# Seven products for eight in one round of a convolutional feed-forward layer, with a factor sum made in place and modulation steps at a shorter pause

## The chip, the cores and the metric

One core of a Trainium2 chip runs the whole program. The time is device microseconds of one execution. Each engine of the core (PE, the multiplying engine; DVE, the vector engine; ACT, the scalar engine; POOL, the general engine; SP, which starts transfers) takes its instructions from a queue of its own, in the order in which the program has them. An instruction waits for semaphores that others raise, and everything behind it on its engine waits too.

## The reference

The program is a small network on one sequence of 512 positions with 1,024 features: a recurrent mixer, a feed-forward layer with a convolution, an attention mixer, a second such feed-forward layer, then a gated feed-forward layer, a hybrid mixer and another gated feed-forward layer. What matters here is the feed-forward layer with a convolution, used twice, its gated sister, and the modulation:

```python
def conv_ffn(h, w_up, conv_w, conv_b, w_down):
    a, v = jnp.split(h @ w_up, 2, axis=-1)
    a = lax.conv_general_dilated(a, conv_w[:, None, :].astype(a.dtype), window_strides=(1,),
                                 padding=[(CONV_W - 1, 0)], dimension_numbers=('NWC', 'WIO', 'NWC'),
                                 feature_group_count=D_FF) + conv_b
    return (jax.nn.silu(a) * v) @ w_down

def swiglu(x, w_gu, w_down):
    g, u = jnp.split(x @ w_gu, 2, axis=-1)
    return (jax.nn.silu(g) * u) @ w_down
...
    for layer in range(DEPTH):
        mod = c_act @ ada_w[layer] + ada_b[layer]
```

The inner width is 2,816, that is 22 tiles of 128; the convolution goes over three positions (the current one and two before it), each feature by itself. All data are 32-bit floats. The modulation of a layer is a vector (the activated condition) times a matrix of 1,024 x 6,144.

## The kernel before

Every large product is made of three products of shorter numbers. A weight block is split on ACT into a high part (line 241) and on DVE into the low part that is left (line 242); the activations are split in the same way (lines 465 and 468). PE adds high x high, high x low and low x high in a bank (lines 354, 355 and 357, called plain below; 455 to 457 where seven products are used).

**Weights.** All blocks of the program stand in one list. SP loads each into one of six slots called raw (512 KB); tasks split it into one of six pairs of buffers, wh and wl, so that up to six split blocks wait for PE. A slot is free when its block has been split.

**Order of the work.** There is no scheduler behind the code. While the Python code emits PE's instructions it adds up a modelled time (`wv.pe`), and side tasks that have come due are run in between and emit theirs: splits, evictions, modulation. A task says with `yield` how many modelled microseconds later it goes on. So where an instruction stands in its engine's queue follows from these delays; when it runs is settled on the chip by the queues and semaphores.

**The feed-forward layers** go over the inner tiles in three rounds, tiles 0 to 6, 6 to 14 and 14 to 22. In each round, pairs of tiles are multiplied up (the a half and the v half), evicted into two buffers mh and ml (the split inner activations), and four blocks of the down product follow. In the convolutional layers a pair is evicted tile by tile: `ev_a` applies the weight of the current position and the bias on ACT (line 1151), adds the two earlier positions on DVE (line 1153) and takes the Silu on ACT (line 1164); `ev_v` multiplies by v (line 1169) and splits.

**Seven products.** In the gated layers from tile 4 on, a pair of tiles is a group of seven products of half the rows and half the positions (`fm_fast`), in place of eight. Positions 0 to 255 and 256 to 511 and the upper and lower half of the 1,024 inputs make a 2 x 2 scheme: of the weights come the factors A11, A12, A22, S1, S2, S3, S4, of the activations the inputs X and the sums T, which `fast_inputs` makes once a layer on DVE (lines 404 and 424 to 427, then a split). S1 is A21 + A22, S2 is S1 + A11, S3 is A11 + A21, S4 is A12 + S2. The products are added in three banks A, E and F; bank A is used by A11, S2, S3 and A22 in turn, and ACT copies it out in between (lines 1111 and 1117). S1 and S3 are summed by loading one block and adding the other with a transfer that accumulates (line 197, issued by POOL); S2 and S4 are summed on DVE (lines 212 and 215), S2 in a buffer of its own.

**Modulation of the second layer** is made during the first convolutional layer by `ada_rest`: for each of twelve column blocks of 512, eight steps on DVE (line 694, then 696), one weight row-block each (loaded by ACT's queue, line 738), each step followed by a pause; four transposes on PE (line 674) and a reduction on DVE (line 676) end the block.

Of the kernel before, what the change touches and what calls it, by code (L numbers as in the profile page):

```python
# [20 lines left out]
S = 512  # L21
# [7 lines left out]
T_D, FAST_FROM, SCRATCH = 1.8, 4, 4096  # L29
# [12 lines left out]
ADA_LAG, ADA_PACE, ADA_START, ADA_PACE0 = 1.8, 2.0, 22.8, 1.5  # L42
# [7 lines left out]

GL_D = (5.0, 4.0, 4.8, 2.2, 2.0)
# [67 lines left out]
class Builder:  # L119
# [35 lines left out]
    FACTORS = ("A11", "A12", "S2", "S1", "S3", "S4", "A22")  # L155

    def w_init(self, items):
        self.loads, self.pieces, self.item_pieces = [], [], []
        self.groups = {}
        for it in items:  # L160
            first = len(self.pieces)
            if it[0] == "S":
# [5 lines left out]
                self.loads += [(a21, a22), (a11,), (a12,), (a11, a21), (a22,)]  # L168
# [17 lines left out]
    def w_dma(self):  # L186

        while self.w_dma_i < len(self.loads) and self.w_dma_i < self.w_freed + RAW_BUFS:
            i = self.w_dma_i
            self.w_dma_i += 1  # L190
            raw = self.t([128, 4, 256], "raw", RAW_BUFS)
            for n, (ap, r0, nk, c0, ncol) in enumerate(self.loads[i]):
                src = ap[r0 * 128:(r0 + nk) * 128, c0:c0 + ncol].rearrange("(k p) m -> p k m", p=128)
                if n == 0:
                    self.nc.sync.dma_start(raw[:, :nk, :ncol], src)
                else:
                    self.nc.gpsimd.dma_start(raw[:, :nk, :ncol], src, accum_op=OP.add)
            self.w_raw[i] = raw

# [4 lines left out]
    PARTS = dict(S1=0, A11=1, A12=2, S3=3, A22=4, S4=2)  # L204

    def w_sum(self, g, name):
# [3 lines left out]
        if name == "S2":  # L210
            g["S2"] = self.t([128, 4, 256], "wsum")
            tt(g["S2"], raw("S1"), raw("A11"), op=OP.add)
            self.raw_free()
        else:
            tt(raw("A12"), raw("A12"), g["S2"], op=OP.add)
# [5 lines left out]
    def w_split(self, i, slow=True):  # L221
# [8 lines left out]
        else:  # L230
            g = p["g"]
            load = g["load"] + self.PARTS.get(kind, 0)
            yield from self.w_wait_load(load)
            src = g["S2"] if kind == "S2" else self.w_raw[load]
# [12 lines left out]
        if kind in ("raw", "S1", "S3", "S4", "A22"):  # L247
            self.raw_free()
        elif kind == "A11":
            self.w_sum(g, "S2")  # L250
        elif kind == "A12":
            self.w_sum(g, "S4")
# [142 lines left out]
    def fast_inputs(self, X, tags, first, second):  # L395
# [12 lines left out]
        def run():  # L408
            yield from self.wv.wait_in(first)
            yield 1.5  # L410
# [22 lines left out]
    def fm_fast(self, X, T, blocks, after):  # L433
# [4 lines left out]
        steps = (("A11", x(0, 0), "A"), ("A12", x(4, 0), "F"), ("S2", t(4, 0), "A"), ("S1", t(0, 0), "E"),  # L438
# [629 lines left out]
    def ffn_blocks(self, up, down, fast=False):  # L1068
        out = []
        for a, b in self.ROUNDS:  # L1070
            for t in range(a, b, 2):
                pair = [(up, 0, 8, t * 128, 256), (up, 0, 8, DFF + t * 128, 256)]
                out += [("S", *pair)] if fast and t >= FAST_FROM else pair
# [3 lines left out]
    def ffn(self, X, waits, up, down, scale, after, conv=None, tags=None):  # L1077
# [4 lines left out]
        fast = tags is not None  # L1082
        if fast:
            T, t_task = self.fast_inputs(X, tags, *waits)
        pend = []

        def fast_group(a, t):
# [42 lines left out]
            self.fm_fast(X, T, ((up, 0, 8, t * 128, 256), (up, 0, 8, DFF + t * 128, 256)), after)  # L1130

        for r, (a, b) in enumerate(self.ROUNDS):
            mh, ml = self.big("b0", F32R), self.big("b1", F32R)
            for t in range(a, b, 2):
# [37 lines left out]
                if fast and t >= FAST_FROM:  # L1172
# [776 lines left out]
    def blocks(self):  # L1949
# [9 lines left out]
        out += self.ffn_blocks(I["ffn_w_up"][0], I["ffn_w_down"][0])  # L1959
# [4 lines left out]
        out += self.ffn_blocks(I["ffn_w_up"][1], I["ffn_w_down"][1])  # L1964
        out += self.ffn_blocks(I["ffn1_w_gu_2"][0], I["ffn1_w_down_2"][0], True)
        out += self.hy_blocks()
        out += self.ffn_blocks(I["ffn2_w_gu_2"][0], I["ffn2_w_down_2"][0], True)
        return out

    def conv_ffn(self, X, waits, layer, after):  # L1970
# [3 lines left out]
        self.ffn(X, waits, I["ffn_w_up"][layer], I["ffn_w_down"][layer], self.m(layer, 5), after, (cw, cb))  # L1974
# [35 lines left out]
    def build(self, stop=99):  # L2010
# [55 lines left out]
        self.conv_ffn(st["X"], st["tasks"], 0, begin1)  # L2066
# [13 lines left out]
        self.conv_ffn(st["X"], st["tasks"], 1, begin2)  # L2080
        if stop == 4:
            for t in self.st2["tasks"]:
# [4 lines left out]
                 tags=("b2", "b3"))  # L2087
# [11 lines left out]
        def begin_out():  # L2099
# [4 lines left out]
            def after(lo, hi):  # L2104
# [3 lines left out]
                 tags=("b2", "b3"))  # L2108
# [22 lines left out]
```

## Time and profile before

| | |
|---|---|
| median of three runs | 2736.74 us (2731.54 to 2738.49) |
| the profiled execution | 2735.41 us |
| its span | 2733.7 us |
| mean granted clock of PE | 0.994 |
| PE busy | 2685.7 us, 98% |
| DVE busy | 1637.7 us, 60% |
| ACT busy | 1143.7 us, 42% |
| POOL busy | 325.2 us, 12% |

The span is the time between the first and the last event that the profiler saw; the execution's own time is a little longer. Of the stages that the change touches, the first convolutional layer goes from about 378 to 760 us: up products of round one until 446, of round two from 480 to 568, of round three from about 615 to 703, each followed by down products. The gated layers go from about 1485 to 1838 and from 2380 to the end. In a timeline row the number behind the shape is the count, and the bracket holds the idle time of the engine just before and what ended it. In a grouped row the sum and the mean in ns stand before the last bar, and behind it the idle time and what ended most of it.

### The profile page before, as it was taken

To read this page: it belongs to the slowest core of one execution; us is meant where nothing else is said; L and a number is where in the kernel's file an instruction comes from. 1 tells how busy PE (TensorE), PEld (TensorE's weight loads), DVE (VectorE), ACT (ScalarE), POOL (GpSimd) and SP (SyncE) were. 2 spreads that over 40 slices of the span, in tenths; PEclk is the share of its full clock that TensorE was granted. 3 is DMA by queue.
4 is the path that set the end of the run, shared out by engine and by line. 5 is a ranking of instruction groups with operands and counts; after the bars stand their busy time and mean duration, and the time that the engine had idled before them with its cause. 6 is when DMAs were issued, how large, how long until landed. Compare 5 with 4: busy or idle time off the path is not lost.

```text
span 2733.7 us, 40282 instructions
## 1 busy us (share of the span) xinstructions
PE 2685.7 (98%) x15857; PEld 2346.6 (86%) x15857; DVE 1637.7 (60%) x2945; ACT 1143.7 (42%) x2114; POOL 325.2 (12%) x440
## 2 busy tenths in 40 slices
PE   6999999999999999999999999999999999999999
PEld 5988898888877888888889898997878987989898
DVE  7866567767553797644446774753456234577574
ACT  3323343323333696433234443543256333344353
POOL 3111110000101594000002000010000000101001
PEclk8999999999999999999999999999999999999999
DMA  7642126565241002232332564747535432357461
GB/s 265 187 152 86 55 67 209 177 189 172 85 116 62 9 2 63 72 114 93 93 99 70 142 168 128 184 69 116 98 81 82 72 82 88 85 139 170 131 171 54
DMA packets 286170, 307.25 MB, mean 112 GB/s; under 512 B 17272, under 2 KB 260365, under 8 KB 285981
## 3 DMA queue, kind: packets, MB, share of 16 engines
q1 hardware_dynamic: 239243, 242.67, 32.2%
q10 hardware_dynamic: 27730, 43.14, 5.2%
q0 software_dynamic: 19008, 18.88, 4.7%
q8 instruction: 125, 2.05, 0.3%
q14 instruction: 64, 0.52, 0.1%
HBM read 302.54 MB, written 2.10 MB: 111 GB/s over the span
## 4 chain that ended last, share of the span: by engine, by line
PE 91%; DVE 5%; ACT 2%; issue 1%; POOL 1%; ACTq 0%; DVEq 0%; POOLq 0%
PE pg L354 21%; PE pg L355 21%; PE pg L357 21%; PE pg L456 4%; PE pg L457 4%; PE pg L455 4%; PE pa L883 2%; PE pg L386 1%; PE pg L384 1%; PE pg L385 1%; PE pa L1488 1%; DVE w L696 1%; DVE wl L242 1%; PE pa L510 1%; DVE w L526 1%
## 5 line engine op out<-in xcount | busy, mean ns | idle before, releaser
L242 DVE TENSOR_TENSOR wl<-raw,wh 128x512 fp32r<-128x512 f32 (+2 forms) x824 | 613.5, 770 | 337.6 <-ACT wh L241 336.3
L354 PE MATMUL pg<-b,wh 128*128 128x512 f32 (+1 forms) x1856 | 673.4, 364 | 1.0 <-DVE w L1169 1.0
L355 PE MATMUL pg<-b,wl 128*128 128x512 f32 (+1 forms) x1856 | 668.1, 361 | 0.0
L241 ACT ACTIVATE wh<-raw 128x512 fp32r<-128x512 f32 (+2 forms) x824 | 515.8, 667 | 300.3 <-PE pg L357 136.9
L357 PE MATMUL pg<-b,wh 128*128 128x512 f32 (+1 forms) x1472 | 522.5, 357 | 0.0
L354 PE MATMUL pg<-hTh,wh 128*128 128x512 f32 (+2 forms) x1096 | 410.9, 377 | 2.4 <-ACT hTh L465 1.2
L355 PE MATMUL pg<-hTh,wl 128*128 128x512 f32 (+2 forms) x1096 | 405.1, 371 | 0.7 <-DVE wl L242 0.7
L354 PEld LDWEIGHTS pg<-b,wh 128*128 128x128 f32 x1856 | 348.6, 188 | 57.1 <-DVE w L1169 1.4
L357 PE MATMUL pg<-hTl,wh 128*128 128x512 f32 (+2 forms) x1096 | 396.3, 368 | 0.0
L355 PEld LDWEIGHTS pg<-b,wl 128*128 128x128 f32 x1856 | 348.8, 188 | 54.6
L357 PEld LDWEIGHTS pg<-b,wh 128*128 128x128 f32 x1472 | 275.1, 188 | 43.7
L354 PEld LDWEIGHTS pg<-hTh,wh 128*128 128x128 f32 (+1 forms) x1096 | 205.5, 187 | 46.6 <-issue 4.6
L357 PEld LDWEIGHTS pg<-hTl,wh 128*128 128x128 f32 (+1 forms) x1096 | 202.3, 187 | 40.6 <-DVE hTl L468 0.4
L355 PEld LDWEIGHTS pg<-hTh,wl 128*128 128x128 f32 (+1 forms) x1096 | 205.5, 187 | 35.6 <-DVE wl L242 1.1
L487 POOL TENSOR_TENSOR w<-w,w 128x256 f32<-128x256 f32 (+1 forms) x78 | 78.0, 1005 | 1222.6 <-ACT w L486 1222.0
L455 PE MATMUL pg<-b,wh 128*128 128x256 f32 x576 | 160.9, 279 | 1.3 <-ACT w L1111 1.3
L457 PE MATMUL pg<-b,wl 128*128 128x256 f32 x576 | 161.3, 280 | 0.0
L456 PE MATMUL pg<-b,wh 128*128 128x256 f32 x576 | 160.7, 279 | 0.0
L465 ACT ACTIVATE b<-w 128x512 fp32r<-128x512 f32 (+1 forms) x92 | 54.4, 594 | 235.8 <-DVE w L1169 149.7
L357 PE MATMUL pg<-hTh,wh 128*128 128x512 f32 (+1 forms) x384 | 142.9, 378 | 0.0
L456 PE MATMUL pg<-hTl,wh 128*128 128x256 f32 x432 | 122.6, 284 | 0.0
L455 PE MATMUL pg<-hTh,wh 128*128 128x256 f32 x432 | 121.3, 281 | 0.0
(414 smaller groups left out, 4218.0 us busy)
## 6 DMA issues: line engine op xcount, KB each, us to landing
raw<-in_ffn_w_gu_dram SPq DMA_DIRECT2D x106, 512.0 KB
raw<-in_ffn_w_up_dram SPq DMA_DIRECT2D x88, 512.0 KB
w<-in_ada_w_dram ACTq DMA_DIRECT2D x160, 256.0 KB
raw<-in_ffn_w_down_dram SPq DMA_DIRECT2D x64, 512.0 KB
raw<-in_w_in_dram SPq DMA_DIRECT2D x64, 512.0 KB
raw<-in_ffn_w_gu_dram POOLq DMA_DIRECT2D x36, 512.0 KB, 6.5
raw<-in_hg_w_in_dram SPq DMA_DIRECT2D x32, 512.0 KB
raw<-in_ffn_w_down_dram SPq DMA_DIRECT2D x32, 384.0 KB
```

Of the source, the lines that this page charges most:

```text
L241: nc.scalar.activation(h[:, k:e, :ncol], src[:, k:e, :ncol], AF.Copy)
L242: nc.vector.tensor_tensor(l[:, k:e, :ncol], src[:, k:e, :ncol], h[:, k:e, :ncol].bitcast(F32), op=OP.subtract)
L354: mm(p[:mw, :n], h[:, c], xh[:, k, lo:hi], start=k == 0, stop=False)
L355: mm(p[:mw, :n], l[:, c], xh[:, k, lo:hi], start=False, stop=False)
L357: mm(p[:mw, :n], at(j)[0][:, c], xl[:, j, lo:hi], start=False, stop=j == nk - 1)
L384: mm(p[:, :n], xh[:, k, tk], h[:, :n], start=k == 0, stop=False)
L455: mm(o, h[:, k, c], xh, start=first and k == 0 and m == 0, stop=False, skip_group_check=True)
L456: mm(o, h[:, k, c], xl, start=False, stop=False, skip_group_check=True)
L457: mm(o, l[:, k, c], xh, start=False, stop=k == 3 and m == 1, skip_group_check=True)
L465: self.nc.scalar.activation(h, src, AF.Copy)
L487: nc.gpsimd.tensor_tensor(acc[0][:, lo:hi], acc[0][:, lo:hi], sq[:, lo:hi], op=OP.add)
L883: mm(p[:, c, :n], s["k"][:, cc], q, start=True, stop=True)
```

## The change

It does four things.

The first convolutional layer's third round (tiles 14 to 22, four groups) uses seven products. `FAST_FROM` is now a table by layer. The eviction of such a group is new: `after_conv` adds the parts of a in a buffer, `convolve` applies the convolution to both tiles, and `out_conv` gates and splits. The sums T of this layer are made later in the layer by a delay of 190 modelled us.

In all groups of seven the order of the factors is A11, S1, S2, A12, S3, S4, A22, and products and weights follow it. S2 is summed in S1's slot; A21 is then added to A11's slot by an accumulating transfer, which makes S3 there. A group loads four slots and six blocks, where it was five slots and seven blocks.

The modulation's pause is 1.3 modelled us for 2.0.

```diff
-T_D, FAST_FROM, SCRATCH = 1.8, 4, 4096
+T_D, SCRATCH = 1.8, 4096
-ADA_LAG, ADA_PACE, ADA_START, ADA_PACE0 = 1.8, 2.0, 22.8, 1.5
+ADA_LAG, ADA_PACE, ADA_START, ADA_PACE0 = 1.8, 1.3, 22.8, 1.5
+FAST_FROM = (14, None, 4, 4)
+T_DELAY = 190.0
...
-    FACTORS = ("A11", "A12", "S2", "S1", "S3", "S4", "A22")
+    FACTORS = ("A11", "S1", "S2", "A12", "S3", "S4", "A22")
...
-                self.loads += [(a21, a22), (a11,), (a12,), (a11, a21), (a22,)]
+                g["a21"] = a21
+                self.loads += [(a21, a22), (a11,), (a12,), (a22,)]
...
+    def w_load(self, raw, block, add=False):
+        ap, r0, nk, c0, ncol = block
+        src = ap[r0 * 128:(r0 + nk) * 128, c0:c0 + ncol].rearrange("(k p) m -> p k m", p=128)
+        if add:
+            self.nc.gpsimd.dma_start(raw[:, :nk, :ncol], src, accum_op=OP.add)
+        else:
+            self.nc.sync.dma_start(raw[:, :nk, :ncol], src)
...
-    PARTS = dict(S1=0, A11=1, A12=2, S3=3, A22=4, S4=2)
+    PARTS = dict(S1=0, A11=1, A12=2, A22=3, S2=0, S3=1, S4=2)
...
         if name == "S2":
-            g["S2"] = self.t([128, 4, 256], "wsum")
-            tt(g["S2"], raw("S1"), raw("A11"), op=OP.add)
-            self.raw_free()
-        else:
-            tt(raw("A12"), raw("A12"), g["S2"], op=OP.add)
+            tt(raw("S1"), raw("S1"), raw("A11"), op=OP.add)
+            self.w_load(raw("A11"), g["a21"], True)
+        else:
+            tt(raw("A12"), raw("A12"), raw("S2"), op=OP.add)
+            self.raw_free()
...
-        steps = (("A11", x(0, 0), "A"), ("A12", x(4, 0), "F"), ("S2", t(4, 0), "A"), ("S1", t(0, 0), "E"),
+        steps = (("A11", x(0, 0), "A"), ("S1", t(0, 0), "E"), ("S2", t(4, 0), "A"), ("A12", x(4, 0), "F"),
                  ("S3", t(0, 256), "A"), ("S4", x(4, 256), "E"), ("A22", t(4, 256), "A"))
...
+            def convolve():
+                x, y = c["a"], c["y"]
+                w = lambda j, m: cw[:, j * FT + t + m:j * FT + t + m + 1]
+                yield 1.0
+                for m in range(2):
+                    nc.scalar.activation(y[:, m], x[:, m], AF.Identity, scale=w(2, m), bias=cb[:, t + m:t + m + 1])
+                yield 1.6
+                for m in range(2):
+                    for j, d in ((1, 1), (0, 2)):
+                        nc.vector.scalar_tensor_tensor(y[:, m, d:], x[:, m, :S - d], w(j, m), y[:, m, d:],
+                                                       op0=OP.mult, op1=OP.add)
+                    yield 1.7
+                nc.scalar.activation(y, y, AF.Silu)
+                yield 1.8
+                hi = y[:, :, 256:512]
+                nc.vector.scalar_tensor_tensor(hi, hi, -1.0, two(c["5"]), op0=OP.mult, op1=OP.mult)
+
+            def out_conv(A):
+                y = c["y"]
+                yield from self.wv.wait_in(c["task"])
+                lo = y[:, :, 0:256]
+                nc.vector.scalar_tensor_tensor(lo, lo, -1.0, two(A), op0=OP.mult, op1=OP.mult)
+                yield 0.9
+                nc.scalar.activation(mh[:, f, :], y, AF.Copy)
+                yield 1.6
+                nc.vector.tensor_tensor(ml[:, f, :], y, mh[:, f, :].bitcast(F32), op=OP.subtract)
+
+            def after_conv(step, banks):
+                A, E, F = (banks.get(n) for n in "AEF")
+                if step in ("A11", "S1", "S2", "S3"):
+                    return after(step, banks)
+                if step == "A12":
+                    c["a"] = self.t([128, 2, 512], "hmask")
+                    nc.vector.tensor_tensor(c["a"][:, :, 0:256], two(c["1"]), two(F), op=OP.add)
+                elif step == "S4":
+                    c["y"] = self.t([128, 2, 512], "cy")
+                    nc.vector.tensor_tensor(c["a"][:, :, 256:512], two(c["2"]), two(E), op=OP.add)
+                    c["task"] = self.wv.spawn(convolve())
+                    pend.append(c["task"])
+                else:
+                    pend.append(self.wv.spawn(out_conv(A)))
```

The order on the engines, first ACT in round three of the first convolutional layer before the change: the splits of weights (241), the two tiles of a pair (1151, 1164) and loads of the modulation (738).

```order
L241 ACTIVATE wh_877_5776<-raw_841_5547 128x512
L1151 ACTIVATE w2_880_5781<-pg_871_5737,PT_8_77 128x512
L1164 ACTIVATE w2_879_5780<-w2_880_5781 128x512
L738 DMA w2_882_5791<-in_ada_w_dram 128x512
L241 ACTIVATE wh_877_5776<-raw_841_5547 128x512
L738 DMA w2_883_5808<-in_ada_w_dram 128x512
L1151 ACTIVATE w2_886_5822<-pg_881_5786,PT_8_77 128x512
L1164 ACTIVATE w2_885_5821<-w2_886_5822 128x512
```

Now ACT in the same round after the change, from the high split of S3 of the third group (in the slot raw_873) to the high split of the next group's S1 (raw_892). cy_909 is the second group's convolution output (1143, then Silu in 1150 and the last copy in 1161); w2_916, w2_920 and w2_923 are the third group's copies of A11, S1 and S2 (1118, 1121, 1124).

```order
L249 ACTIVATE wh_910_5970<-raw_873_5588 128x1024
L1143 ACTIVATE cy_909_5965<-hmask_903_5903,PT_8_77 128x512 x2
L249 ACTIVATE wh_913_6002<-raw_885_5712 128x1024
L1118 ACTIVATE w2_916_6033<-pg_860_5538 128x512
L249 ACTIVATE wh_917_6038<-raw_889_5744 128x1024
L1150 ACTIVATE cy_909_5965<-cy_909_5965 128x1024
L1121 ACTIVATE w2_920_6066<-pg_862_5540 128x512
L249 ACTIVATE wh_921_6071<-raw_896_5813 128x1024
L1161 ACTIVATE b0_858_5536<-cy_909_5965 128x1024
L1124 ACTIVATE w2_923_6099<-pg_860_5538 128x512
L249 ACTIVATE wh_924_6104<-raw_892_5776 128x1024
```

The evictions of one group now stand between the copies of the next group's banks, and in front of its splits.

DVE in the same stretch after the change, from the third group's low split of S3 to the sum S2 of the fourth (219).

```order
L250 TENSOR_TENSOR wl_911_5971<-raw_873_5588,wh_910_5970 128x1024
L250 TENSOR_TENSOR wl_914_6003<-raw_885_5712,wh_913_6002 128x1024
L1147 SCALAR_TENSOR_TENSOR cy_909_5965<-hmask_903_5903,PT_8_77,cy_909_5965 128x511
L1147 SCALAR_TENSOR_TENSOR cy_909_5965<-hmask_903_5903,PT_8_77,cy_909_5965 128x510
L1147 SCALAR_TENSOR_TENSOR cy_909_5965<-hmask_903_5903,PT_8_77,cy_909_5965 128x511
L1147 SCALAR_TENSOR_TENSOR cy_909_5965<-hmask_903_5903,PT_8_77,cy_909_5965 128x510
L250 TENSOR_TENSOR wl_918_6039<-raw_889_5744,wh_917_6038 128x1024
L250 TENSOR_TENSOR wl_922_6072<-raw_896_5813,wh_921_6071 128x1024
L1153 SCALAR_TENSOR_TENSOR cy_909_5965<-cy_909_5965,w2_897_5837 128x2x256
L1159 SCALAR_TENSOR_TENSOR cy_909_5965<-cy_909_5965,pg_860_5538 128x2x256
L250 TENSOR_TENSOR wl_925_6105<-raw_892_5776,wh_924_6104 128x1024
L219 TENSOR_TENSOR raw_892_5776<-raw_892_5776,raw_896_5813 128x1024
```

The whole convolution of the second group (1147 to 1159) stands between the third group's S3 and the fourth group's sum, where before the change two steps a tile stood behind the tile's bank.

DVE in the first gated layer, before the change: the sums S2 in the buffer wsum (212) and S4 (215), and the splits around them.

```order
L242 TENSOR_TENSOR wl_2014_14505<-raw_1993_14283,wh_2013_14504 128x1024
L212 TENSOR_TENSOR wsum_2015_14508<-raw_1989_14249,raw_1993_14283 128x1024
L242 TENSOR_TENSOR wl_2019_14540<-raw_2002_14376,wh_2018_14539 128x1024
L215 TENSOR_TENSOR raw_2002_14376<-raw_2002_14376,wsum_2015_14508 128x1024
L242 TENSOR_TENSOR wl_2022_14571<-wsum_2015_14508,wh_2021_14570 128x1024
L1122 TENSOR_TENSOR w2_2020_14565<-w2_2020_14565,pg_1953_13971 128x512
```

And after: raw_1995 is A11's slot, raw_1991 that of S1, raw_2006 that of A12.

```order
L250 TENSOR_TENSOR wl_2019_14650<-raw_1995_14396,wh_2018_14649 128x1024
L250 TENSOR_TENSOR wl_2022_14680<-raw_1991_14369,wh_2021_14679 128x1024
L219 TENSOR_TENSOR raw_1991_14369<-raw_1991_14369,raw_1995_14396 128x1024
L1126 TENSOR_TENSOR w2_2013_14612<-w2_2013_14612,pg_1985_14349 128x512
L250 TENSOR_TENSOR wl_2024_14711<-raw_1991_14369,wh_2023_14710 128x1024
L1129 TENSOR_TENSOR w2_2017_14644<-w2_2017_14644,pg_1983_14347 128x512
L250 TENSOR_TENSOR wl_2026_14741<-raw_2006_14520,wh_2025_14740 128x1024
L222 TENSOR_TENSOR raw_2006_14520<-raw_2006_14520,raw_1991_14369 128x1024
L1131 TENSOR_TENSOR w2_2020_14674<-w2_2020_14674,pg_1984_14348 128x512
L250 TENSOR_TENSOR wl_2029_14773<-raw_1995_14396,wh_2028_14772 128x1024
```

The sum S2 (219) stands after the split of S1, with S4 (222) two splits later; the split of S3 in the last row reads A11's slot, which the accumulating transfer has changed between.

## Rows read from the trace of the kernel before

**Rows 1.** The page: busy time, share of the span and instructions of each engine, and the engines' shares of the chain of waits that ended last.
```profile
PE 2685.7 (98%) x15857; PEld 2346.6 (86%) x15857; DVE 1637.7 (60%) x2945; ACT 1143.7 (42%) x2114; POOL 325.2 (12%) x440
PE 91%; DVE 5%; ACT 2%; issue 1%; POOL 1%; ACTq 0%; DVEq 0%; POOLq 0%
```

**Rows 2.** Windows: the stretch in us, its length, busy time and instruction count of PE, of PE's weight loads, DVE, ACT and POOL, then PE's granted clock, the share in which the transfer engines were busy, and GB/s. In this order: first layer's modulation; down products of round one; down products of round two; a group of round three; after a wait of PE; a wait of PE in the first gated layer; a group of seven products there.
```profile
110.00:155.00 45.00, 45.00 (x386) 45.00 (x385) 30.62 (x53) 14.57 (x31) 1.35 (x2) 1.00 0.71 222
440.00:460.00 20.00, 20.00 (x91) 16.45 (x90) 13.63 (x24) 5.96 (x14) 0.00 (x0) 1.00 0.76 236
569.00:613.00 44.00, 44.00 (x198) 36.16 (x197) 28.31 (x46) 9.64 (x17) 0.00 (x0) 1.00 0.62 195
617.00:639.40 22.40, 22.40 (x101) 18.41 (x100) 14.66 (x24) 6.51 (x11) 0.00 (x0) 1.00 0.50 148
786.80:790.20 3.40, 3.40 (x10) 2.67 (x9) 1.43 (x3) 1.53 (x3) 0.00 (x0) 0.51 0.50 134
1525.00:1535.00 10.00, 8.73 (x68) 8.21 (x67) 8.34 (x10) 6.48 (x9) 0.00 (x0) 1.00 0.17 52
1604.00:1623.80 19.80, 19.80 (x169) 19.80 (x169) 15.40 (x17) 10.89 (x15) 2.60 (x2) 1.00 0.78 187
```

**Rows 3.** Timeline of ACT in round three: the first tile's eviction of two neighbouring pairs.
```profile
643.73 0.78 ACT L1151 ACTIVATE w<-pg,PT 128x512 f32<-128x512 f32 x1 [2.58 <-PE pg L357]
666.16 0.78 ACT L1151 ACTIVATE w<-pg,PT 128x512 f32<-128x512 f32 x1 [2.58 <-PE pg L357]
```

**Rows 4.** Timeline of PE at a block's transposes, and the plain product after them.
```profile
703.50 0.60 PE L674 MATMUL pa<-ident,w 128*128 128x128 f32 x4
703.85 0.48 PE L354 MATMUL pg<-b,wh 128*128 128x512 f32 x1
```

**Rows 5.** Timeline of ACT over a group of seven products in the first gated layer.
```profile
1603.79 0.60 ACT L1111 ACTIVATE w<-pg 128x512 f32<-128x512 f32 x1 [0.81 <-PE pg L457]
1604.29 1.05 ACT L241 ACTIVATE wh<-raw 128x1024 fp32r<-128x1024 f32 x1
...
1615.06 1.06 ACT L241 ACTIVATE wh<-raw 128x1024 fp32r<-128x1024 f32 x1 [1.21 <-issue]
1617.91 1.06 ACT L241 ACTIVATE wh<-raw 128x1024 fp32r<-128x1024 f32 x1 [1.79 <-PE pg L456]
...
1620.75 1.06 ACT L241 ACTIVATE wh<-raw 128x1024 fp32r<-128x1024 f32 x1 [1.26 <-PE pg L456]
...
1623.66 0.60 ACT L1111 ACTIVATE w<-pg 128x512 f32<-128x512 f32 x1 [0.81 <-PE pg L457]
```

**Rows 6.** Timeline of DVE in the same layer: at 1513 to 1519 the sums T, from 1603 one group.
```profile
1513.00 0.69 DVE L404 TENSOR_TENSOR w<-hTh,hTl 128x512 f32<-128x512 f32 x1
...
1518.27 0.42 DVE L424 TENSOR_TENSOR w<-w,w 128x256 f32<-128x256 f32 x1
...
1603.11 1.29 DVE L1105 TENSOR_TENSOR b<-w,b 128x512 fp32r<-128x512 f32 x2
...
1607.67 1.23 DVE L242 TENSOR_TENSOR wl<-raw,wh 128x1024 fp32r<-128x1024 f32 x1 [0.34 <-ACT wh L241]
1608.82 1.22 DVE L212 TENSOR_TENSOR wsum<-raw,raw 128x1024 f32<-128x1024 f32 x1
...
1612.31 1.23 DVE L215 TENSOR_TENSOR raw<-raw,wsum 128x1024 f32<-128x1024 f32 x1
...
1620.81 0.69 DVE L1128 SCALAR_TENSOR_TENSOR w<-w,pg 128x512 f32<-128x512 f32 x1
```

**Rows 7.** Groups of instructions by line: three of 612 to 700 us (round three), and the modulation steps of 108.8 to 155.4 us (21 of them).
```profile
L1153 DVE SCALAR_TENSOR_TENSOR w<-pg,PT,w 128x511 f32<-128x511 f32 (+1 forms) x16 | 12.0, 750 | 10.5 <-ACT w L1151 10.2
L696 DVE SCALAR_TENSOR_TENSOR w<-w,cact,w 128x512 f32<-128x512 f32 x27 | 20.1, 746 | 0.1
L1164 ACT ACTIVATE w<-w 128x512 f32<-128x512 f32 x8 | 5.1, 632 | 13.2 <-DVE w L1153 8.3 <-DMA raw<-in_ffn_w_up_dram 3.3 <-DMA raw<-in_ffn_w_down_dram 1.7
L696 DVE SCALAR_TENSOR_TENSOR w<-w,cact,w 128x512 f32<-128x512 f32 x21 | 15.7, 748 | 2.4 <-DMA w<-in_ada_w_dram 2.0
```

**Rows 8.** Timeline of POOL in the same group of the gated layer: an accumulating transfer is issued when the sum of line 215 is done.
```profile
1613.62 1.29 POOL L197 DMA_DIRECT2D raw<-in_ffn_w_gu_dram  x1 [7.73 <-DVE raw L215]
```

**Rows 9.** All instructions of line 197: durations (min, median, max, in ns), and us from issue to landing.
```profile
L197 POOL DMA_DIRECT2D raw<-in_ffn_w_gu_dram x36: 1282/1292/1452, 1481.6 to 2642.4; - x36
...
DMA to landing us min/median/max: 5.7/6.5/8.3
```

**Rows 10.** Timeline of PE after its two longer waits.
```profile
785.26 0.44 PE L1313 MATMUL pa<-ident,w 48*128 48x48 f32 x4 [1.50 <-ACT w L1307]
1533.60 0.38 PE L455 MATMUL pg<-b,wh 128*128 128x256 f32 x1 [1.27 <-ACT w L1111]
```

**Rows 11.** PE's idle time in front of all transposes of line 674, by what ended it: us, times.
```profile
  DVE w L696: 0.5, 1
```

More of the change, by code (lines that the diff above doesn't have):

```diff
@@ L191, in w_dma @@
             raw = self.t([128, 4, 256], "raw", RAW_BUFS)
[L192 to L195, printed above, removed]
-                else:
-                    self.nc.gpsimd.dma_start(raw[:, :nk, :ncol], src, accum_op=OP.add)
-            self.w_raw[i] = raw
+            for n, block in enumerate(self.loads[i]):
+                self.w_load(raw, block, n > 0)
+            self.w_raw[i] = raw
+    def w_load(self, raw, block, add=False):
[5 more added lines that the diff above has]
+            self.nc.sync.dma_start(raw[:, :nk, :ncol], src)
     def raw_free(self, n=1):
@@ L390, in tm, with fast_inputs @@
                 self.w_done(got[j].pieces)
-    def fast_inputs(self, X, tags, first, second):
+    def fast_inputs(self, X, tags, first, second, delay):
         nc = self.nc
@@ L1066, with ffn_blocks @@
     ROUNDS = ((0, 6), (6, 14), (14, 22))
-    def ffn_blocks(self, up, down, fast=False):
+    def ffn_blocks(self, up, down, fast=None):
         out = []
@@ L1072, in ffn_blocks, with ffn @@
                 pair = [(up, 0, 8, t * 128, 256), (up, 0, 8, DFF + t * 128, 256)]
-                out += [("S", *pair)] if fast and t >= FAST_FROM else pair
+                out += [("S", *pair)] if fast is not None and t >= fast else pair
             out += [(down, a, b - a, i * 256, 256) for i in range(4)]
         return out
-    def ffn(self, X, waits, up, down, scale, after, conv=None, tags=None):
+    def ffn(self, X, waits, up, down, scale, after, fast, tags, conv=None):
         nc = self.nc
@@ L1081, in ffn @@
             cw, cb = conv
-        fast = tags is not None
-        if fast:
-            T, t_task = self.fast_inputs(X, tags, *waits)
+        if fast is not None:
+            T, t_task = self.fast_inputs(X, tags, *waits, T_DELAY if fast > 8 else 0.0)
         pend = []
@@ L1132, in ffn @@
+            self.fm_fast(X, T, ((up, 0, 8, t * 128, 256), (up, 0, 8, DFF + t * 128, 256)),
+                         after if conv is None else after_conv)
         for r, (a, b) in enumerate(self.ROUNDS):
@@ L1171, in ffn @@
                 first = r == 0 and t == a
-                if fast and t >= FAST_FROM:
+                if fast is not None and t >= fast:
                     self.wv.wait(t_task)
@@ L1973, in conv_ffn @@
         cb = self.P("ffn_conv_b", layer * 22, 22)
-        self.ffn(X, waits, I["ffn_w_up"][layer], I["ffn_w_down"][layer], self.m(layer, 5), after, (cw, cb))
+        self.ffn(X, waits, I["ffn_w_up"][layer], I["ffn_w_down"][layer], self.m(layer, 5), after,
+                 FAST_FROM[layer], tags, (cw, cb))
     def load_x(self):
```

30 lines of the change are left out of this document (14 added, 16 removed).

## The prediction

> **What bounds the kernel now.** I read the page's busy shares and its chain of waits first [rows 1]: the multiplying engine (PE) is busy for 98% of the 2733.7 us span and carries 91% of the chain, so an edit pays only if it takes work off PE, and costs only if it makes PE wait. The profiled execution took 2735.41 us, 1.7 us more than its span and 1.33 us under the median of the three runs shown, 2736.74. I work against the first and add 1.33 at the end.
>
> Then I read windows over single stages [rows 2]. In round three of the first convolutional layer PE is busy without a gap (22.40 of 22.40 us) while the vector engine (DVE) does 14.66. Where seven products already run (the first gated layer) PE is gapless too, with DVE at 15.40 of 19.80 and the scalar engine (ACT) at 10.89. So DVE has a quarter of its time free there, and the question for a new user of seven products is what DVE and ACT must do in turn inside a group's shorter PE time.
>
> **Part 1, seven products in round three.** Removed: the ACT copies of two plain groups start 22.43 us apart (643.73, 666.16) [rows 3]. One modulation transpose falls into such a group and holds PE .35 us (703.50 to 703.85) [rows 4], so a plain group is 22.08. In the gated layer the copies of A11 start 1603.79 and 1623.66 [rows 5]: 19.87 a group, 2.84 a product. Four groups save 4 x 2.21 = 8.85 us, all on PE, if nothing waits.
>
> Added: inputs for the second half of the products (sums of the activations, 8 ops of .69, 16 of .42, 8 low splits of .69 on DVE (1513.00, 1518.27) [rows 6], 5.5 + 6.7 + 5.5 = 17.7 us). They stand beside round two's down products, where DVE is busy 28.31 of 44.00 us [rows 2], some 13 of them modulation (two blocks of 6.6) that part 3 moves ahead; 15 + 17.7 leave 11 us free. I count nothing; without that cover the splits would be late for round three's first product by what DVE lacks.
>
> On DVE each group now has seven splits of 1.23, two factor sums of 1.22, three sums of bank parts and two gates of .69, four convolution steps of .75 and a low part of 1.29 [rows 6, 7]: 8.6 + 2.4 + 3.5 + 3.0 + 1.3 = 18.8 of 19.87 us, or 95%. By its share DVE just keeps up. The order is the matter. The order fences of the change show a ring between two groups. PE's fifth product (S3) of group g+1 adds in the bank that holds S2, so it waits for ACT's copy of S2 (line 1124). ACT issues that copy only after group g's last copy (1161), which waits for DVE's 1159, which stands behind the convolution of g, which stands behind the split of factor S3 of g+1, whose raw data the new accumulating transfer brings, which starts after DVE's sum (219) of g+1. Behind the S2 copy stand the splits of the next S1, and behind them the next sum (219).
>
> I walk this ring from the end of one sum (219), with each op at the trace's duration. The transfer starts .1 us later (sum ends 1613.54, transfer 1613.62) and lands after 6.5 [rows 8, 9]: 6.6. High split of S3 on ACT, 1.05: 7.65. Two bias steps on ACT, by the Silu of that width .63 [rows 7], less the .1 by which ACT's neighbours overlap (1603.79 + .60 against 1604.29) [rows 5]: 8.7. High split of S4: 9.8; its low split on DVE: 11.0. Four convolution steps: 14.0. Silu of 1,024 columns, estimated at the 1.05 of a split of that width: 15.0. S1's bank copy, then the high split of the next A11: 16.5; its low split: 17.7. Upper gate and lower gate: 19.04. Last copy, 1.05: 20.1. S2's copy: 20.7. High split of next S1: 21.65; low split: 22.85; next sum, 1.23: 24.1. So the ring turns in 24.1 us where PE needs 19.87.
>
> When does it catch PE? In the first group nothing is before it. ACT copies S2 of group 1 as PE ends its third product, 3 x 2.84 + .6 = 9.1; the split of S1 and the sum follow (1.05, 1.23, 1.23 and hops): 12.7. The S2 copy of group 2 then ends at 12.7 + 20.7 = 33.4, and PE is there at 19.87 + 4 x 2.84 = 31.2: a wait of 2.2. Groups 3 and 4 each lose 24.1 - 19.87 = 4.25 more. Together 10.7, so round three comes out at -8.85 + 10.7 = +1.9.
>
> The ring's links bound this. Landing at 5.7, the lowest of the 36 [rows 9]: waits of 8.3, round three -.5. At 8.3, the highest: first wait 4.0, then 6.0 each, 16.0, round three +7.2. If the transfer cost nothing, DVE's own order (the sum, a low part, two sums, two splits between) would make the split of S3 no earlier than 7.1 after the sum, the ring 23.0, waits 7.0, round three -1.85. I take 6.5, the median.
>
> The Trainium skill, "DMA: Bandwidth & Descriptors", section "Anatomy of one DMA — SWDGE (gpsimd) path", gives a fit of about 2 us plus the bytes over 436 GB/s; for 512 KB that is an estimate of 3.2 us, and by it the transfer would not be a link and round three would be -1.85. The trace differs: 5.7 at least in 36 [rows 9], and the measurement decides. "SBUF — State Buffer" has a trap by which some vector operations hold back descriptors that GpSimd writes; if it held here, with DVE at 95%, landing would move to the 8.3 end.
>
> **Part 2, factor order and sum in place, in all groups.** In the 18 gated groups PE's work is the same. Transfers fall from seven to six blocks of 512 KB a group; PE waits for none there, so I count no gain. What is new is a wait: S3's low split comes after the accumulating transfer, where the old order had both blocks summed long before. The sum would end where that of line 212 ends now, 1608.82 + 1.22 = 1610.04, and land at 1616.6; the fifth split of the group now starts at 1615.06, so S3's is 1.6 late, done at 1617.7, and the next one starts at 1617.91 as before [rows 5, 6]. The ring closes inside a group, as no convolution stands in it. A landing at 8.3 leaves ACT 1.6 us behind at 1619.5, against idle of 1.26 and .81 before the next copy of A11 [rows 5]; should DVE's share of the delay spend the last of these, a pair loses .8. For 12 pairs of neighbours within a round that is 0 to +10, and I take +.5. The one wait of PE for line 1111, 1.27 us at 1533.60 [rows 10], stays.
>
> **Part 3, modulation at a shorter pause.** A column block issues the same eight vector steps of .75, a reduction of .69 and four transposes, before with 105 matmuls of other work to a block, after with 60: at 22.08 / 96 = .23 us each that is a block in 24.2 us, then 13.8. No PE work changes. DVE, at 13.63 of 20.00 in round one [rows 2], that is .68, carries 6.6 / 24.2 = .27 for it; .41 + 6.6 / 13.8 = .89 after. The first layer's modulation ran about this densely, 21 later steps or three blocks in 46.6 us: PE 45.00 of 45.00, DMA .71 [rows 2], and its steps waited for their data 2.0 us in all [rows 7]; in the whole run PE waited for such a step once, .5 us [rows 11]. Bounds 0 and +6 (a dozen blocks at .5); nearer the low: +1. In return modulation ends near 576 us, so none is left in round three.
>
> **Clock.** After PE's idle 1.50 us at 785.26, the granted clock was .51 over 786.80 to 790.20, the lower level of 1.2 GHz; after 1.27 us idle at 1533.60 it stayed 1.00 [rows 2, 10]. Three waits of 2 to 4 us in a row may bring some of this: a half clock of 3.4 us costs 1.7, thus 0 to 5; I take +1. The Trainium skill, "TensorE: Matmul & The Clock Gate", section "HAM oscillation — how this bites in real kernels", says that pauses between bursts bring the clock down; by it each of the three waits would cost, +5 rather than +1.
>
> **Sum.** -8.85 + 10.7 + .5 + 1 + 1 = +4.4: 2739.8 for a profiled execution, 2741.1 against the median.
>
> **Rivals.** *A, the ring doesn't bind*: the S2 copy is on time because ACT and DVE run ahead of my walk (as in the gated layer, whose group has no convolution and closes). For it: 95% is under 100%, and six split factors are kept ahead of PE. Against: the ring's ops are in-order and each has a row. Then -8.85 with nothing else: 2727.9. *B, slower*: the accumulating transfers land late in round three because loads for round three's down products run beside; place: the split of S3 of groups 2 to 4; price +7.2 at a landing of 8.3, with clock falls of 5 and the other terms 1.5: +13.7, 2750.4. It decides from a landing of about 7.5 on. *C, the change's transfer is late in the gated layers*: 12 pairs at .8, +10 over the round-three result of +1.9 and the other 2: 2750.6. *D, round three doesn't run as the diff says* has no support: the fences show the seven products.
>
> **How the numbers follow.** 0.3% is 8.2 us, about what a measurement of this kernel can tell from no change: faster is under 2728.5, slower over 2744.9. Chances: forecast .55, A .20, B .15, C .10. The forecast's own range is 2736 to 2748 (landing 5.7 and nothing else, to half-way to B's landing with clock losses); .08 of all cases are in it over 2744.9. Faster takes three quarters of A, whose time is only .6 under the bound: .15. Slower takes B, most of C and that .08: .30; same .55. Range 2727 to 2751: A stands at its low end, B and C at its high.
>
> **What would show it.** Round three's PE windows: three waits before S3's products on line 1124, near 2.2, 4.2 and 4.2 us, the first in group 2. None of them: A. Landing over 7.5 us: B. PE waits for line 1118 or a split of S3 in the gated layers: C. DVE busy below 85% of round three without those waits, or modulation's transposes making PE wait over 6 us, would make my terms wrong.

## The result, and the profile after

The changed kernel takes 2751.57 us (median of 4 runs, 2750.04 to 2756.37) against 2737.22 before: ratio 1.0070, interval 1.0058 to 1.0082, that is 16 to 22 us slower. The forecast was 2741.1 in a range of 2727 to 2751, with "no change" as the likeliest outcome.

The page of the changed kernel, busy time by engine, answers to the first of [rows 1].

```profile
PE 2683.5 (98%) x16145; PEld 2356.6 (86%) x16145; DVE 1674.6 (61%) x2989; ACT 1162.4 (42%) x2122; POOL 336.0 (12%) x448
```

PE is busy 2.2 us less in a span that is 15.7 us longer (2749.4 for 2733.7). PE's own waits over the whole changed run say more (engine, tile and line, what it waited for, us in total, times, longest):

```profile
PE pa L682 <- DVE w L704: 10.7, 7, 3.8
...
PE pg L463 <- ACT w L1124: 6.5, 3, 3.4
```

Line 682 holds the modulation's transposes (674 before), which in the whole run before waited for a vector step once, .5 us [rows 11]; line 1124 is the copy of S2, the ring of the prediction.

Windows cut at PE's own first instructions give the place. In the kernel before, rounds one and two of the first convolutional layer, then round three up; the columns as in [rows 2].

```profile
377.86:615.61 237.75, 237.25 (x1152) 198.68 (x1151) 163.69 (x281) 83.67 (x153) 0.74 (x1) 1.00 0.57 176
615.61:705.32 89.71, 89.71 (x402) 73.69 (x400) 63.18 (x99) 31.47 (x53) 0.00 (x0) 1.00 0.54 164
```

The same two stretches in the changed kernel:

```profile
375.73:631.03 255.30, 243.95 (x1168) 201.93 (x1167) 202.91 (x347) 88.61 (x156) 4.76 (x4) 0.99 0.61 190
631.03:721.75 90.72, 84.23 (x674) 83.62 (x672) 65.32 (x74) 45.58 (x57) 6.42 (x5) 0.94 0.53 134
```

Rounds one and two take 17.55 us more. Four blocks of transposes that stood in round three now stand here, 4 x .35 = 1.4, so 16.1 us are lost. Round three takes 90.72 for 89.71 - 1.4 = 88.3, that is +2.4. The layer is 18.6 us longer (416.7 for 398.1), and its start came 2.1 us earlier in this execution. So most of the loss sits where the prediction had put one microsecond.

### The profile page after: what moved, and what is told of

Read it like the earlier page. It is cut to its first block, busy times and chain, and to the rows that moved or that the text cites. A ratio compares the mean times of both kernels' runs of the same rounds, so it can differ in the third digit from the quotient of the medians.

```text
span 2749.4 us, 40943 instructions
## 1 busy us (share of the span) xinstructions
PE 2683.5 (98%) x16145; PEld 2356.6 (86%) x16145; DVE 1674.6 (61%) x2989; ACT 1162.4 (42%) x2122; POOL 336.0 (12%) x448
## 4 chain that ended last, share of the span: by engine, by line
PE 69%; DVE 5%; ACT 2%; DMA 1%; issue 1%; POOL 0%; ACTq 0%; DVEq 0%; POOLq 0%
PE pg L362 16%; PE pg L363 16%; PE pg L365 16%; PE pg L464 5%; PE pg L465 4%; PE pg L463 4%; PE pa L1538 1%; PE pg L394 1%; PE pg L393 1%; PE pg L392 1%; DVE wl L250 1%; DMA raw<-in_ffn_w_up_dram 1%; PE pa L1307 1%; PE pa L1581 1%; PE pa L1422 1%
## 5 line engine op out<-in xcount | busy, mean ns | idle before, releaser
L250 DVE TENSOR_TENSOR wl<-raw,wh 128x512 fp32r<-128x512 f32 (+2 forms) x838 | 646.2, 797 | 376.3 <-ACT wh L249 375.1
L249 ACT ACTIVATE wh<-raw 128x512 fp32r<-128x512 f32 (+2 forms) x838 | 545.4, 690 | 333.7 <-PE pg L365 137.2
L362 PE MATMUL pg<-b,wh 128*128 128x512 f32 (+1 forms) x1728 | 623.3, 362 | 1.0 <-DVE w L1219 1.0
L363 PE MATMUL pg<-b,wl 128*128 128x512 f32 (+1 forms) x1728 | 620.3, 360 | 0.0
L365 PE MATMUL pg<-b,wh 128*128 128x512 f32 (+1 forms) x1344 | 473.5, 354 | 0.0
L362 PEld LDWEIGHTS pg<-b,wh 128*128 128x128 f32 x1728 | 325.4, 188 | 53.3 <-DVE w L1219 1.4
L365 PEld LDWEIGHTS pg<-b,wh 128*128 128x128 f32 x1344 | 251.7, 188 | 37.7
L463 PE MATMUL pg<-b,wh 128*128 128x256 f32 x672 | 187.9, 280 | 1.4 <-ACT w L1118 1.4
L465 PE MATMUL pg<-b,wl 128*128 128x256 f32 x672 | 188.1, 280 | 0.0
L464 PE MATMUL pg<-b,wh 128*128 128x256 f32 x672 | 187.5, 279 | 0.0
L463 PE MATMUL pg<-hTh,wh 128*128 128x256 f32 x560 | 159.3, 285 | 6.5 <-ACT w L1124 6.5
L464 PE MATMUL pg<-hTl,wh 128*128 128x256 f32 x560 | 160.9, 287 | 0.0
L465 PE MATMUL pg<-hTh,wl 128*128 128x256 f32 x560 | 158.8, 284 | 0.0
```

The costliest lines, as they stand in the source:

```text
L249: nc.scalar.activation(h[:, k:e, :ncol], src[:, k:e, :ncol], AF.Copy)
L250: nc.vector.tensor_tensor(l[:, k:e, :ncol], src[:, k:e, :ncol], h[:, k:e, :ncol].bitcast(F32), op=OP.subtract)
L362: mm(p[:mw, :n], h[:, c], xh[:, k, lo:hi], start=k == 0, stop=False)
L363: mm(p[:mw, :n], l[:, c], xh[:, k, lo:hi], start=False, stop=False)
L365: mm(p[:mw, :n], at(j)[0][:, c], xl[:, j, lo:hi], start=False, stop=j == nk - 1)
L463: mm(o, h[:, k, c], xh, start=first and k == 0 and m == 0, stop=False, skip_group_check=True)
```

## The experiments

**e1, the shorter pause alone**, in the kernel before.

```diff
-ADA_LAG, ADA_PACE, ADA_START, ADA_PACE0 = 1.8, 2.0, 22.8, 1.5
+ADA_LAG, ADA_PACE, ADA_START, ADA_PACE0 = 1.8, 1.3, 22.8, 1.5
```

> The kernel before with the modulation's pause at 1.3 for 2.0 and nothing else. Theory M (the shorter pause makes transposes wait on PE for the vector engine's last step, and the clock falls after the longer waits): about 10 us or more slower than before, transposes waiting 6 us or more in all. Rival T (the time before round three was lost to the sums of the activations and the new loads, which share DVE with the modulation): within 4 us of before, transposes waiting under 2 us in all.

Ratio 1.0034 (1.0021 to 1.0048), 9 us slower. The whole layer, and a window over the first waiting transposes, in this run (line 674 still):

```profile
377.20:784.90 407.70, 400.52 (x2056) 339.19 (x2055) 267.73 (x465) 143.97 (x266) 11.48 (x16) 1.00 0.48 152
420.00:430.00 10.00, 6.22 (x23) 4.80 (x23) 8.32 (x15) 2.05 (x4) 0.00 (x0) 0.85 0.77 250
```

Its waits, by PE's list:

```profile
PE pa L674 <- DVE w L696: 6.4, 5, 3.8
```

The layer was 398.1 before, so the pause alone costs 9.6 us in it. PE's idle time at the transposes is 6.4 of this. Counted from the start of the product before to the start of a block's transposes, less the .23 us of an undisturbed block, the stops come to 7.8, as PE's records overlap (703.50 + .60 against 703.85 [rows 4]) and a short stop doesn't show as idle. The lower clock after the longest wait is worth some 1.5 us more (granted clock .85 over ten us). Theory M holds for more than half of the 16 us, and T is refuted as the only cause.

**e2, factor order and sum in place alone**: the changed kernel with two lines put back.

```diff
-FAST_FROM = (14, None, 4, 4)
+FAST_FROM = (None, None, 4, 4)
-ADA_LAG, ADA_PACE, ADA_START, ADA_PACE0 = 1.8, 1.3, 22.8, 1.5
+ADA_LAG, ADA_PACE, ADA_START, ADA_PACE0 = 1.8, 2.0, 22.8, 1.5
```

> The changed kernel with a plain round three and the pause at 2.0, so that the new factor order and the sum in place in the gated layers are all that is left of the change. My prediction's term: +.5 us, at most +10. Theory M: within 2 us of before, with PE's waits in the gated layers as before (one near 1.3 us). Rival C of the prediction: 5 to 10 us slower.

Ratio 1.0002 (.9993 to 1.0011), that is from 2 us faster to 3 us slower. In the gated layers PE waits once for line 1118, 1.4 us, where it waited 1.27 for the same copy before. ACT does wait for the accumulating transfer, 39.3 us in ten places, without making PE wait longer:

```profile
  ACT wh L249: 39.3, 10
...
DMA to landing us min/median/max: 5.7/5.9/8.0
```

Rival C falls. Part 2 costs nothing that can be told from zero.

**e7, the pause put back, the rest of the change kept.**

```diff
-ADA_LAG, ADA_PACE, ADA_START, ADA_PACE0 = 1.8, 1.3, 22.8, 1.5
+ADA_LAG, ADA_PACE, ADA_START, ADA_PACE0 = 1.8, 2.0, 22.8, 1.5
```

> The changed kernel with the modulation's pause back at 2.0. Theory M: the first two rounds lose nothing (237 to 240 us for 255.3), but five blocks of modulation then stand in round three, 6.6 us of DVE in each 24, and the ring of round three, already 25.0 us, turns more slowly by what of it falls into the ring's DVE links, 2 to 4 us a turn: round three 97 to 103 us for 90.7, the whole 5 to 10 us under the changed kernel and 5 to 12 over the one before. Rival (the pause is not to blame, the sums of the activations are): the first two rounds stay above 248 us.

Ratio 1.0065 (1.0051 to 1.0079): as slow as the changed kernel, where 5 to 10 us less had been expected, but in the other place:

```profile
378.05:615.79 237.74, 237.12 (x1152) 198.57 (x1151) 175.80 (x302) 85.62 (x153) 4.76 (x4) 1.00 0.57 174
615.79:719.00 103.21, 87.97 (x689) 86.17 (x688) 88.62 (x116) 47.02 (x60) 6.45 (x5) 0.93 0.68 187
```

Rounds one and two lose nothing, though the sums T are built in them: T and round three's loads cost nothing at the old pause, the pause alone 9.6 us, both together 16.1. Round three, which holds its four blocks of transposes again, takes 103.21 us for 89.71. DVE does 88.62 us there, the copies of line 1124 start 27.15 us apart (655.25, 682.40), and PE's waits for them are 11.6 us for 6.5. So at the old pause the modulation costs its time in round three, where its steps stand between those of the ring.

**e3, transposes later**: at the shorter pause, each block's transposes go into a task of their own some 4 modelled us later.

```diff
-            self.ada_cols(layer, j, [acc], pai)
+            if layer:
+                last = self.wv.spawn(cols(j, acc), ADA_LATE)
+            else:
+                self.ada_cols(layer, j, [acc], pai)
             yield 0.5
```

> The changed kernel with each block's four transposes put some 4 modelled us later, in a task of their own, so that the vector steps keep their pace. Theory M-lead (DVE can do the work at this pace, only the transposes stand too close behind the last step): their waits, 11 us, and the clock lost after them, 5 us, go, so about 16 us under the changed kernel, near 2736. Rival M-full (at this pace DVE falls further and further behind, so that a later place does not help): more than half of the 11 us of waits stays, 2745 or more.

Ratio 1.0019 (1.0010 to 1.0028), 14 us better than the changed kernel. Rounds one and two, then round three:

```profile
376.03:616.68 240.65, 239.40 (x1168) 199.88 (x1167) 202.08 (x347) 87.81 (x156) 4.76 (x4) 1.00 0.65 202
616.68:706.35 89.67, 82.16 (x673) 81.34 (x672) 65.33 (x74) 45.35 (x57) 6.42 (x5) 0.98 0.53 136
```

No transposes of this layer make PE idle any more. 240.65 less 1.4 for the four blocks moved is 1.5 us over before, with the same 202 us of DVE work in less time. So theory M-lead holds: DVE could do the work at this pause; it was only done too late for where the transposes stood. Round three is left as it was: PE still waits 6.5 us for the copy of S2. DVE at the first block of the changed kernel, and PE's transposes after it:

```profile
422.46 0.68 DVE L1219 TENSOR_TENSOR w<-w,pg 128x512 f32<-128x512 f32 x1
423.83 0.69 DVE L476 TENSOR_TENSOR b<-w,b 128x512 fp32r<-128x512 f32 x1 [0.69 <-ACT b L473]
424.44 0.74 DVE L704 SCALAR_TENSOR_TENSOR w<-w,cact,w 128x512 f32<-128x512 f32 x1
```

```profile
425.24 0.94 PE L682 MATMUL pa<-ident,w 128*128 128x128 f32 x4 [3.79 <-DVE w L704]
```

The block's last step (424.44) stands behind the gate of the pair (1219) and a low split (476) that itself waits for ACT. In the kernel before the same block's last step was done 2.4 us ahead of the transposes (430.61 + .74 against 433.74); over all twelve blocks this lead is 2.3 to 5.2 us there:

```profile
430.61 0.74 DVE L696 SCALAR_TENSOR_TENSOR w<-w,cact,w 128x512 f32<-128x512 f32 x1
...
433.74 0.60 PE L674 MATMUL pa<-ident,w 128*128 128x128 f32 x4
```

**e6, three loads ahead** for two, to tell late loads from a late DVE.

```diff
         load()
         load()
+        if layer:
+            load()
```

> The changed kernel with three of the modulation's loads ahead of the vector steps for two. Theory D (where transposes wait, the vector steps stand behind other work of DVE): the waits before the first and the seventh block (3.95 and 1.73 us) stay; only the last one (3.32 us), in front of which DVE itself waits 2.2 us for a load, goes; 3 to 5 us under the changed kernel. Rival L (the loads are late everywhere, as ACT issues them behind its own waits): all five waits go, 11 to 16 us under it.

Ratio 1.0047 (1.0034 to 1.0061). The wait before the last block is gone, those before the first (4.25 us at 428.46) and the seventh (1.65) stay, and two of .76 and .94 between them and the last fall to .16 or less. Rounds one and two take 248.91 for 255.30:

```profile
428.46 0.66 PE L682 MATMUL pa<-ident,w 128*128 128x128 f32 x4 [4.25 <-DVE w L704]
```

So both happen: late vector steps at the first and the seventh block, a late load before the last, and loads have a part in the smaller waits. ACT issues these loads, and in the changed kernel it issued that one behind a split that had waited 4.58 us for DVE:

```profile
584.29 0.63 ACT L473 ACTIVATE b<-w 128x512 fp32r<-128x512 f32 x1 [4.58 <-DVE w L1219]
584.30 0.33 ACTq L746 DMA_DIRECT2D w<-in_ada_w_dram  x1
```

In e1, which has neither round three's loads nor the sums T, this last wait isn't there; which of them brings it on wasn't tried.

**e4, the last copy behind the next group's S2 copy.**

```diff
-                yield 0.9
+                yield 3.4
                 nc.scalar.activation(mh[:, f, :], y, AF.Copy)
```

> The changed kernel with ACT's last copy of a convolved group some 2.5 modelled us later, so that it stands behind the next group's copy of S2 and the high split of its successor's S1. Theory R (the ring of the prediction is what PE waits for in round three): the ring turns in about 21.5 us for 25.0, the three waits of 6.5 us in all fall to 2 us or less, the half clock in round three goes, round three takes 80 to 83 us for 90.7, the whole about 8 us under the changed kernel. Rival (the waits come from late accumulating transfers, wherever the copy stands): waits of 4 us or more stay.

Ratio 1.0044 (1.0028 to 1.0060). Round three, and the first of the copies that had been late:

```profile
633.96:716.81 82.85, 80.06 (x674) 79.66 (x672) 64.88 (x73) 45.56 (x57) 6.42 (x5) 1.00 0.58 146
```

```profile
663.33 0.59 ACT L1124 ACTIVATE w<-pg 128x512 f32<-128x512 f32 x1
...
684.80 0.59 ACT L1124 ACTIVATE w<-pg 128x512 f32<-128x512 f32 x1
```

21.5 us from copy to copy, the number expected; no wait for line 1124 is left, the clock is at 1.00, and 7.9 us come back. The waits left, 2.8 us, are for a sum (1129) that stands on DVE behind the low part (1163) of the group before.

**e8, S3 in a slot of its own** in round three, added ahead of time; one load a group more.

```diff
+                g["own"] = len(self.groups) <= 4
-                self.loads += [(a21, a22), (a11,), (a12,), (a22,)]
+                self.loads += [(a21, a22), (a11,), (a12,)] + ([(a11, a21)] if g["own"] else []) + [(a22,)]
...
-            self.w_load(raw("A11"), g["a21"], True)
+            if g["own"]:
+                self.raw_free()
+            else:
+                self.w_load(raw("A11"), g["a21"], True)
```

> The changed kernel with S3 of round three's four groups loaded into a slot of its own (A11 and A21 added there ahead of time, as the kernel before did it in the gated layers), so that no transfer stands in the ring; loads and sums are else the same. Theory R: the ring then turns at DVE's own order, 23 to 24 us for 25.0; the split of S3 no longer waits for a transfer, waits before line 1124's product fall from 6.5 to 3 to 5 us, round three 86 to 89 us for 90.7. Rival (the accumulating transfer alone makes the waits): no waits, round three near 80.

Ratio 1.0058 (1.0045 to 1.0072). The copies (line 1132 here) start 23.3 us apart, PE's waits for them are 3.7 us, round three takes 86.53:

```profile
664.68 0.58 ACT L1132 ACTIVATE w<-pg 128x512 f32<-128x512 f32 x1
...
688.00 0.58 ACT L1132 ACTIVATE w<-pg 128x512 f32<-128x512 f32 x1
```

The transfer was a link of the ring, worth about 1.7 us a turn; the place of the last copy, 3.5 us a turn in e4, was the larger one. The prediction's sum for a transfer that costs nothing had a turn of 23.0 us and round three at -1.85; measured are 23.3 and 86.53 - 88.3 = -1.8.

**e5, both repairs** (e3 and e4, the low part of the split later too).

```diff
-                yield 1.6
+                yield 3.4
                 nc.vector.tensor_tensor(ml[:, f, :], y, mh[:, f, :].bitcast(F32), op=OP.subtract)
```

> The changed kernel with both repairs: transposes 4 modelled us later in a task of their own, and ACT's last copy of a convolved group behind the next group's S2 copy (its low part later too). Theory M-lead with R: the first two rounds as in the run with late transposes alone, 240.7 us, round three as with the later copy alone, 82.9 us or a little less, as its last wait stood behind that low part: the layer 394 us for 398.1 before and 416.7 in the changed kernel, the whole 3 to 5 us under the kernel before. Rival (the two stages feed each other, so that what is saved in one is waited for in the other): the same as the kernel before or slower.

Ratio .9989 (.9980 to .9998), 3 us faster than before. Rounds one and two 240.08, round three 81.79, the layer 392.5 for 398.1; of the 5.6 us gained there, 2.7 go again in the attention stage (355.8 us for 353.1), where PE waits 3.24 us for ACT (1.50 before [rows 10]). That stage took 349.4 to 353.9 us in the other runs so far, none of which changes it, so part of the 2.7 may be the spread of single executions:

```profile
781.42 0.66 PE L1373 MATMUL pa<-ident,w 48*128 48x48 f32 x4 [3.24 <-ACT w L1367]
```

**e9, e5 with eight small loads of that stage issued by POOL**, and **e10, the same in the kernel before.** ACT had stood 4.81 us behind them in e5.

```diff
-                    self.nc.scalar.dma_start(w1[i][half * 64:half * 64 + 64], src[:, l0:l0 + 8, :])
+                    self.nc.gpsimd.dma_start(w1[i][half * 64:half * 64 + 64], src[:, l0:l0 + 8, :])
```

> The kernel of e5_both with the attention stage's eight small loads of its compression weights issued by POOL for ACT's queue. In e5_both PE's longest wait left is 3.4 us early in the attention stage, behind ACT, which stands 4 to 5 us at these loads; after it the clock falls. Theory: that wait falls to about 1 us, the clock stays up, the attention stage takes 4 to 6 us less than in e5_both (355.8 us) and the whole is 6 to 9 us under the kernel before. Rival: POOL's issues land as late or are waited for elsewhere: within 2 us of e5_both.

> The kernel before with the same eight loads issued by POOL and nothing else, to tell how much of the run above owes nothing to the change. Theory: PE's wait of 1.5 us goes to under 1 us and the clock stays up there: 2 to 4 us under the kernel before. Rival: no difference within 2 us.

e9: ratio .9975 (.9965 to .9984), 7 us faster than before and some 26 faster than the changed kernel; the wait is gone and the attention stage 8.0 us shorter than in e5, which is more than expected. e10: .9997 (.9988 to 1.0006), nothing that can be told from zero, against what was expected: its wait went too, but the clock fell in the same stage all the same (below).

**e11, the changed kernel once more**, beside e9 and e10.

> The changed kernel as it is, on the chip of the two runs above. As first measured: 14 to 19 us over the kernel before; the first two rounds of the convolutional layer 253 to 258 us, round three 90 to 92.

Ratio 1.0073 (1.0058 to 1.0089); 255.46 and 90.98 us for the two stretches, waits of 10.9 and 6.9 us. The split of the loss repeats.

## Why the prediction was wrong

**The step that failed** is part 3: "Bounds 0 and +6 (a dozen blocks at .5); nearer the low: +1." It measured 16.1, and the prediction's own sign, transposes making PE wait over 6 us, came true. PE stood idle in front of seven of the twelve blocks' transposes, 10.7 us in all, 10.2 of them in five places (3.79, 1.56, .76, .94 and 3.15). Counted from start to start, as in e1, the stops are 12.3. The clock fell behind the two longest, which costs about 3.5 us more (10 us at .83, shown further below, and 26 us at .93):

```profile
590.00:616.00 26.00, 24.11 (x101) 19.77 (x102) 19.76 (x33) 5.30 (x8) 2.57 (x2) 0.93 0.40 102
```

Of the 16.1, 9.6 come with the pause alone (e1) and the rest only with round three's loads and sums beside it (e7).

Three readings led there. The likeness to 110 to 155 us was one of the modulation's density alone; DVE's whole load there was 30.62 of 45.00, .68 [rows 2], not the .89 that I had worked out for the new place in the same paragraph, and no convolution was evicted there. Even so the lead was short there, .34 us before the transposes at 124.79 and 1.6 before those at 140.07 and 155.35, so the trace held the warning:

```profile
123.70 0.75 DVE L696 SCALAR_TENSOR_TENSOR w<-w,cact,w 128x512 f32<-128x512 f32 x1
...
124.79 0.38 PE L674 MATMUL pa<-ident,w 128*128 128x128 f32 x2
```

And I had read how seldom PE waited for a step (.5 us, once [rows 11]), not how near it came: the lead of 2.4 us that a block's last step had at 433.74 was the number to set against what a busier DVE would take from it. A dozen blocks at .5 was no bound, since a single wait can be the length of a stretch of DVE's queue: the first was 3.79.

**Part 1 was right** in its mechanism and its size. The forecast of round three was +1.9 by the ring at the median landing, and it measured +2.4 (90.72 for 88.3). The first S2 copy that is late ended at 664.59, 33.6 us after the round's start, for 33.4; PE's wait there was 2.20 for 2.2. The two later copies ended 58.6 and 82.1 us after the start, for 57.5 and 81.6.

```profile
664.65 0.58 PE L463 MATMUL pg<-hTh,wh 128*128 128x256 f32 x1 [2.20 <-ACT w L1124]
...
689.63 0.58 PE L463 MATMUL pg<-hTh,wh 128*128 128x256 f32 x1 [3.42 <-ACT w L1124]
...
713.13 0.39 PE L463 MATMUL pg<-hTh,wh 128*128 128x256 f32 x1 [0.87 <-ACT w L1124]
```

The ring turned in 25.0 us (664.01 to 689.00) and then in 23.5 (to 712.50) for 24.1. The two later waits are shorter than 4.2 because the clock was down after the first two waits (.94 over the round) and PE itself took the time: its busy time in the round is 84.23 us for the 79.5 of four groups at 19.87. As the ring, on other engines, set the end, the slower PE added nothing here, so my separate +1 for the clock was counted twice in round three and was missing in rounds one and two. DVE's 18.8 us a group, 95%, was too much: neighbours on DVE overlap as those on ACT do (1607.67 + 1.23 against 1608.82 [rows 6]), and DVE is busy 17.7 us in the turn from 664.01, 89% of 19.87. It was the order that bound, as the prediction says and e4 shows. Rival A falls with these waits, and B too: the three transfers in the ring were issued at 644.43, 668.65 and 693.69, and the splits that waited for them started at 650.34, 675.33 and 699.78, so they took 5.9 to 6.7 us.

The rule of the Trainium skill on the clock gate ("TensorE: Matmul & The Clock Gate", "HAM oscillation — how this bites in real kernels"), that pauses between bursts bring the clock down, was borne out by the trace for the longer waits: the granted clock was .83 over the ten us that hold the transposes' wait of 3.79 us, and 1.00 in the same ten us before the change. It was not for each wait: over 512 to 530 us, with the wait of 1.56, and over 712 to 722, with that of .87, the clock was 1.00. I had given it +5 and taken +1. The ten us in the changed kernel:

```profile
420.00:430.00 10.00, 6.21 (x23) 4.80 (x22) 7.55 (x14) 2.16 (x4) 0.00 (x0) 0.83 0.66 218
```

**Part 2 was right at its low end** (e2). **Part 1's cover for the sums T**, DVE's idle time beside round two's down products, held at the old pause (e7).

## What to carry to other kernels

When work is packed more densely, read the lead, the time between the last instruction that feeds a consumer and the consumer, and set it against the queue that may stand in front; counting past waits shows nothing of it. A short consumer on the bound engine should stand well behind its producers in program order; a task of its own did that here and took the layer's waits at the transposes from 10.7 us to none (e3). And walk in-order queues as a ring from group to group: a ring of several engines, each below full, can still turn more slowly than the bound engine.

## What was not expected

The clock also fell where PE did not wait. In e10, with PE's early wait in the attention stage gone, PE was busy 105.00 of 105.00 us, yet the granted clock of the stretch was .93 where before it was .98 with PE at 103.37:

```profile
795.00:900.00 105.00, 105.00 (x480) 81.13 (x479) 45.19 (x83) 30.57 (x57) 12.13 (x22) 0.93 0.20 63
```

```profile
795.00:900.00 105.00, 103.37 (x494) 79.48 (x493) 47.27 (x86) 31.73 (x59) 12.09 (x22) 0.98 0.23 71
```

The stage took 352.9 us there and 353.1 before, so in these two executions what the wait gave back went to the clock. In e10 the clock was 1.00 over 860 to 870 us and .66 over 870 to 875, right behind 32 small products (64 x 32) that stand back to back:

```profile
867.26 3.33 PE L1372 MATMUL pa<-kcp,b 64*128 64x32 f32 x32
```

In the kernel before the same 32 products ran from 870.96, and the clock stayed at 1.00 until 880. So this fall needed no wait, and the same work doesn't bring it each time. What decides stays open.
